# Block, partial-sum, low-part and latent-weight stores moved to GpSimd's queue, and another order of the three products of a block, in a two-layer decoder trunk

## The chip, the cores and the metric

The kernel runs on one core of one Trainium2 chip. The metric is the device time of one execution in microseconds, as the median of the runs shown. In the profile PE is TensorE's matmul, PEld its weight load, DVE is VectorE, ACT is ScalarE, POOL is GpSimd and SP is SyncE, which does nothing here but issue DMAs. PE and PEld share one sequencer.

## The reference

A decoder trunk of two layers works on 1024 tokens of width 1024, in float32. Layer 0 mixes with an mLSTM, layer 1 with latent attention on a shared latent K/V; each mixer is followed by an MLP with a squared ReLU and hidden width 4096. Every sub-block is wrapped in RMS norms, a shift and scale that a conditioning vector gives, and a gated residual. What the change touches most is the MLP and the latent projections:

```python
def sqrelu_mlp(h, w1, w2):
    return jnp.square(jax.nn.relu(h @ w1)) @ w2

def mla_shared_kv(x, shift, scale, g_in, w_a, g_latent, w_b, cos, sin):
    h = modulate(rmsnorm(x, g_in), shift, scale)
    kv = h @ w_a
    c_kv, k_rope = jnp.split(kv, [B_KV_LORA], axis=-1)
    ...
```

## The kernel before

**Split products.** A float32 operand is split into two float32r parts, a high part (a ScalarE copy) and a low part (a VectorE subtraction). `wsplit` (L199 to L206) does that for weights: L202 writes `wh`, L203 writes `wl`, both from the pool tag `ws` with 8 buffers. A product of 128 x 128 weights with 512 columns is then three matmuls into the same PSUM tile, made by `mm3` (L243): low-high (L244), high-low (L245), high-high (L246). Nearly all matrix work goes through `mm3`. Where the tokens' side is stationary (`up_rows`, and the mLSTM projections) `lh, ll` are parts of activations, elsewhere of weights.

**Buffers.** Raw weights come by DMA into the tag `raw` with only 4 buffers of 128 x 1024, each held until its split has read it. `k4` has 24 buffers and holds almost everything of that size, `tmp` has 3 buffers of 128 x 512, `ws` has 8. A buffer that a store reads is free only when the store has landed.

**Stages.** The 1024 tokens are two halves of 512. The first 470 us or so are the mLSTM layer. Then come the MLP of layer 0, the attention of layer 1 and its MLP, woven together. An MLP goes through its weights in three sweeps of 16 steps, so that the second half needs fewer products: a block of products is taken apart into sums, and partial results go through DRAM.

- Sweep 1 (`first`, L952): 128 x 512 of the first half's hidden values per step. The first half of its product is copied to `c` and stored to DRAM as the block sum `m` (L967, 256 KB).
- Sweep 2 (`second`, L976): per step two raw weight tiles are loaded (L983), and `m` is read back into `u` (L988). DVE makes sums and differences of the weights (L990, L991, L992, L997); L994 and L995 write the high and the low part `wv` of one of them, `wsplit` those of another, and the block of differences `o` is stored as `s` (L998, 512 KB). `hid` multiplies `wv` first (L1009), adds the result to `u` (L1010, with two more of the same kind), and stores the partial sums `u` (L1017, 512 KB).
- Sweep 3 (`third`, L1026) reads `s` and `u` back for the second half of the tokens.
- The down projection is `up_cols` (L1133) in layer 0 and `up_rows` in layer 1. `up_cols` stores the low part of its weights for the first half of the tokens as `lo` (L1156, 512 KB) and reads it back for the second half (L1168).
- `latent_weights` (L1327) runs beside layer 0's sweep 2, from about 700 to 830 us. For each of six blocks it loads a raw tile (L1337), accumulates a bias on DVE (L1341 to L1344), multiplies the tile by the gains (L1346), splits it, and stores high and low part as `lw` (L1351 or L1353, 512 KB each; half that for block 2). `latent` reads them back later.

So there are 32 stores each of `m`, `s`, `u` and `lo`, and 12 of `lw`: 140. All other stores of intermediate results stay on SP.

**What sets the order.** The kernel is written as Python generators that are interleaved by hand (`two_streams`, `weave`, `in_turn`). `go` chains them: with `tc.issue_after(last[0])` each piece's TensorE instructions are queued behind those of the piece before, so PE's order is nearly the program's. DVE, ACT, SP and POOL are ordered when the kernel is built: the framework plays the program through a timing model and puts an instruction into its engine's queue when the model has its inputs ready, by priority (`prompt` gives 300 steps of precedence). On the chip each queue then runs strictly in that order, and an instruction that waits holds back what is queued behind it.

```python
    def mm3(o, lh, ll, rh, rl, start, stop):
        nc.tensor.matmul(o, ll, rh, start=start, stop=False)
        nc.tensor.matmul(o, lh, rl, start=False, stop=False)
        pe_last[0] = nc.tensor.matmul(o, lh, rh, start=False, stop=stop)
    ...
                nc.scalar.copy(t[:, l_], r[0][:, l_])
                nc.vector.tensor_sub(t[:, r_], r[0][:, l_], t[:, l_].bitcast(F32))
                w = wsplit(r[1], 1024)
                nc.vector.tensor_sub(o[:, r_], r[0][:, r_], r[0][:, l_])
                nc.sync.dma_start(self.s[p_], o)
```

POOL has little to do before the change: nine small loads at the start (L275), memsets of single columns that claim accumulators (L173, waiting until the buffer is free), and memsets in the softmax (L1555).

Of the kernel before, what the change touches and what calls it, by code (L numbers as in the profile page):

```python
# [9 lines left out]
F32 = mybir.dt.float32  # L10
# [72 lines left out]
def kernel(  # L83
# [27 lines left out]
    nc = tc.nc  # L111
# [20 lines left out]
    def raw(dt=F32):  # L132
        return sb.tile([P, 1024], dt, tag="raw", bufs=RAW, name=f"raw_{next(uid)}")
# [13 lines left out]
    def ps():  # L147
        return pp.tile([P, 512], F32, tag="ps", bufs=2, name=f"ps_{next(uid)}")
# [89 lines left out]
    def wcols(w, c0, n=P, k0=0, nk=KD):  # L238
        return w[k0 * P : (k0 + nk) * P, c0 : c0 + n].rearrange("(k p) n -> p k n", p=P)

    pe_last = [None]

    def mm3(o, lh, ll, rh, rl, start, stop):  # L243
        nc.tensor.matmul(o, ll, rh, start=start, stop=False)  # L244
        nc.tensor.matmul(o, lh, rl, start=False, stop=False)  # L245
        pe_last[0] = nc.tensor.matmul(o, lh, rh, start=False, stop=stop)  # L246


    nc.scalar.preload_act_table_set("natural_log_exp_and_others")
# [672 lines left out]
    class Mlp:  # L922
# [29 lines left out]
        def first(self, p_, h):  # L952

            def load():
                r = raw()
                nc.sync.dma_start(
                    r.rearrange("p (a b) -> p a b", b=P), wcols(self.w1, p_ * P)
                )  # L960
                return wsplit(r, 1024)

            def hid(w):
                pt, c = ps(), tmp()
                self.product(pt, self.part(w, 0), h)
                evac(c, pt)
                nc.sync.dma_start(self.m[p_], c)  # L967
                yield "within"
                pt, s = ps(), tmp()
                self.product(pt, self.part(w, 1), h, 4)  # L970
                prompt(nc.vector.tensor_add)(s, c, pt)
                self.squares(0, p_, s)

            return prompt(load), hid

        def second(self, p_, ops):  # L976

            def load():  # L980
                r = [raw(), raw()]
                for i in range(2):
                    nc.sync.dma_start(  # L983
                        r[i].rearrange("p (a b) -> p a b", b=P),
                        wcols(self.w1, (p_ + NPR * i) * P),
                    )
                u, o = k4()[:, :1024], k4()[:, :1024]
                nc.sync.dma_start(u[:, :512], self.m[p_])  # L988
                l_, r_ = slice(0, 512), slice(512, 1024)
                nc.vector.tensor_add(o[:, l_], r[1][:, l_], r[1][:, r_])  # L990
                nc.vector.tensor_sub(r[1][:, l_], r[0][:, l_], r[1][:, l_])  # L991
                nc.vector.tensor_sub(r[0][:, l_], o[:, l_], r[0][:, l_])  # L992
                t = sb.tile([P, 1024], F32R, tag="ws", bufs=WS, name=f"wv_{next(uid)}")
                nc.scalar.copy(t[:, l_], r[0][:, l_])  # L994
                nc.vector.tensor_sub(t[:, r_], r[0][:, l_], t[:, l_].bitcast(F32))  # L995
                w = wsplit(r[1], 1024)
                nc.vector.tensor_sub(o[:, r_], r[0][:, r_], r[0][:, l_])  # L997
                nc.sync.dma_start(self.s[p_], o)  # L998
                return (t[:, l_], t[:, r_]), w, u

            def hid(ws):
                s2, w, u = ws
                u2, u3 = u[:, 0:512], u[:, 512:1024]
                if 4 not in ops:
                    ops[4] = half_op()
                    for k in range(4):
                        split_mod(ops[4].hi[k], ops[4].lo[k], ops["t4"][k], None)
                pt = ps()
                self.product(pt, s2, ops[2])  # L1009
                prompt(nc.vector.tensor_add)(u2, u2, pt)  # L1010
                if p_ and ops["later"]:
                    ops["later"].pop(0)()
                yield "within"
                pt = pc()
                self.product(pt, self.part(w, 0), ops[3])
                prompt(nc.vector.tensor_add)(u3, u2, pt)
                nc.sync.dma_start(self.u[p_], u)  # L1017
                yield "within"
                pt, s = ps(), tmp()
                self.product(pt, self.part(w, 1), ops[4])  # L1020
                prompt(nc.vector.tensor_add)(s, u3, pt)
                self.squares(0, NPR + p_, s)

            return prompt(load), hid

        def third(self, p_, ops, buf):  # L1026
# [106 lines left out]
        def up_cols(self, half, y, fs, i, last):  # L1133
            G, w2, hids = len(fs), self.w2, self.hids[half]
            n = KD // G

            def out(w):
                for m in range(i * n, (i + 1) * n, 2):
                    if m > i * n:
                        yield "within"  # L1140
                    b2, made = pm(), list(hids)
                    for j, q in enumerate(sorted(range(G), key=lambda q: made.index(fs[q]))):
                        for e in range(2):
                            c_ = ts(m + e - i * n, P)
                            mm3(
                                b2[:, e], w[0][:, q, c_], w[1][:, q, c_], *hids[fs[q]],
                                j == 0, j == G - 1,
                            )
                    self.accumulate((half, m + 1), y.t[m // 2], b2)

            views = [(a, 0, wcols(w2, i * n * P, n * P, f, r)) for a, f, r in self.runs(fs)]

            def load():
                if not half:
                    w = wload(views, n * P)
                    nc.sync.dma_start(self.lo[i][:, fs[0] : fs[0] + G], w[1].bitcast(F32))  # L1156
                    return w
                r = raw()
                w = [
                    sb.tile([P, 1024], F32R, tag="ws", bufs=WS, name=f"wk_{next(uid)}").rearrange(  # L1160
                        "p (a b) -> p a b", b=n * P
                    )
                    for _ in range(2)
                ]
                rv = r.rearrange("p (a b) -> p a b", b=n * P)
                for a, f, k in self.runs(fs):
                    nc.sync.dma_start(rv[:, a : a + k], wcols(w2, i * n * P, n * P, f, k))
                    nc.sync.dma_start(w[1][:, a : a + k].bitcast(F32), self.lo[i][:, f : f + k])  # L1168
                nc.scalar.copy(w[0], rv)
                return w  # L1170

            return prompt(load), out
# [151 lines left out]
    lw = scratch([6, 2, P, D], "lw")  # L1324
    lbias = const([P, 6 + 112], F32, "lbias")

    def latent_weights():  # L1327

        v = wcols(kv_w_a, 256, 64)
        views = [[(0, wcols(kv_w_a, m * P))] for m in range(2)] + [[(0, v), (64, v)]]  # L1330
        views += [[(0, wcols(b_w_q_a[0], m * P))] for m in range(3)]
        for b, vs in enumerate(views):
            A, sh = (Akv, kvada[:, 0:8]) if b < 3 else (Aq, adac(1, SH1))
            r_ = raw()
            r = r_.rearrange("p (a b) -> p a b", b=P)
            for c0, v in vs:
                nc.sync.dma_start(r[:, :, c0 : c0 + v.shape[2]], v)  # L1337
            yield
            acc = tma()[:, :P]
            with paced():  # L1340
                nc.vector.tensor_scalar(acc, r[:, 0], sh[:, 0:1], None, ALU.mult)  # L1341
                for k in range(1, KD):
                    nc.vector.scalar_tensor_tensor(
                        acc, r[:, k], sh[:, k : k + 1], acc, ALU.mult, ALU.add  # L1344
                    )
            nc.vector.tensor_mul(r, r, A.unsqueeze(2).to_broadcast([P, KD, P]))  # L1346
            for i, t in enumerate(wsplit(r_, D)):
                if b == 2:

                    f = lambda t: t.rearrange("p (a b) -> p a b", b=P)[:, :, ts(i, 64)]  # L1350
                    nc.sync.dma_start(f(lw[b, 0]), f(t).bitcast(F32))  # L1351
                else:
                    nc.sync.dma_start(lw[b, i], t.bitcast(F32))  # L1353
            yield "wait"
            pt = pc()
            nc.tensor.transpose(pt[:, :P], acc, ident)
            n = 64 if b == 2 else P
            nc.vector.reduce_sum(lbias[:n, b : b + 1], pt[:n, :P], axis=AX.X)
            if n < P:
                nc.vector.memset(lbias[n:P, b : b + 1], 0.0)  # L1360
# [797 lines left out]
    u = p0.scaled(xT0, (0,))  # L2158
# [28 lines left out]
    u = p1.scaled(xT0, (0, 1))  # L2187
# [18 lines left out]
    u = p2.scaled(xT0, (0, 1))  # L2206
# [387 lines left out]
```

## Time and profile before

| what | value |
|---|---|
| median of 3 runs (lowest to highest) | 2388.77 us (2384.43 to 2389.36) |
| profiled execution, its own time | 2390.72 us |
| its span, first to last instruction | 2388.9 us |
| mean granted TensorE clock | 0.985 |
| busy: PE, DVE, ACT, POOL | 2281.3, 1675.5, 1085.7, 17.6 us |
| DMA traffic | 482.03 MB, 202 GB/s over the span |

The profile is of one execution. Busy times are unions of an engine's instructions. A wait is charged to what ended last before the waiting instruction. A row of a timeline reads: start, duration, engine, line, operation, what it writes and reads, and in brackets the idle time of the engine just before with what ended it. A row of the waits reads: total in us, how many, the longest. A row of a stretch gives its length, then each engine's busy time and number of instructions, then the granted clock, the share of the DMA engines and GB/s. Matmuls overlap: one lasts about 0.39 us and the next starts well before it ends.

### The profile page before, as it was taken

How to read it: one execution, taken by the hardware profiler on the slowest of the kernel's cores; microseconds unless marked ns; L12 is line 12 of the kernel's file. 1: busy time of each engine (PE TensorE's matmuls, PEld its weight loads, DVE VectorE, ACT ScalarE, POOL GpSimd, SP SyncE). 2: the span in 40 equal slices, each digit the busy share in tenths (PEclk: the TensorE clock that was granted, in tenths of full speed). 3: DMA queues.
4: the chain of work that ended last, by engine and by line, in shares of the span. 5: the costliest groups of instructions: out<-in, count | busy, mean ns of one | idle time of the engine just before them, and what ended most of it. 6: DMA issues, size and time to landing. Idle time of an engine off the chain costs nothing.

```text
span 2388.9 us, 31122 instructions
## 1 busy us (share of the span) xinstructions
PE 2281.3 (95%) x11274; PEld 1886.1 (79%) x11274; DVE 1675.5 (70%) x2745; ACT 1085.7 (45%) x1811; POOL 17.6 (1%) x95
## 2 busy tenths in 40 slices
PE   8999999999998999999999989999999799999998
PEld 6888888887776788778878768878778688878887
DVE  6666767799887877767764787656648876666556
ACT  4364335574332335544444454534446333454433
POOL 1000000000000000000000000000000000000000
PEclk9999999999999999999999999999999899999999
DMA  9544455667998987655675774945246587675321
GB/s 319 171 131 123 150 151 158 190 210 240 300 280 256 297 270 273 210 185 176 194 242 160 268 236 135 323 166 187 104 138 233 151 275 224 222 262 187 115 90 69
DMA packets 406267, 482.03 MB, mean 202 GB/s; under 512 B 30468, under 2 KB 276289, under 8 KB 406113
## 3 DMA queue, kind: packets, MB, share of 16 engines
q1 hardware_dynamic: 405824, 479.94, 62.3%
q8 instruction: 89, 1.46, 0.3%
q14 instruction: 66, 0.53, 0.1%
q0 software_dynamic: 288, 0.10, 0.0%
HBM read 358.33 MB, written 121.63 MB: 201 GB/s over the span
## 4 chain that ended last, share of the span: by engine, by line
PE 73%; DVE 12%; DMA 9%; ACT 3%; issue 2%; SPq 1%; DVEq 0%; ACTq 0%
PE ps L244 12%; PE ps L245 12%; PE ps L246 12%; PE pm L244 8%; PE pm L245 8%; PE pm L246 8%; DMA raw<-in_mlp_w_dram 4%; DVE wl L203 2%; PE pc L245 2%; PE pc L244 2%; PE pc L246 2%; DVE k L211 1%; ACT wh L202 1%; DVE hd L458 1%; DVE tma L348 1%
## 5 line engine op out<-in xcount | busy, mean ns | idle before, releaser
L202 ACT CAST wh<-raw 128x1024 fp32r<-128x1024 f32 (+4 forms) x307 | 310.5, 1014 | 471.6 <-PE pm L245 119.8
L203 DVE TENSOR_TENSOR wl<-raw,wh 128x1024 fp32r<-128x1024 f32 (+4 forms) x307 | 360.9, 1178 | 220.8 <-ACT wh L202 198.8
L244 PE MATMUL ps<-k,wl 128*128 128x512 f32 x1100 | 436.7, 397 | 12.8 <-DVE wl L203 5.8
L245 PE MATMUL ps<-k,wh 128*128 128x512 f32 x1100 | 430.9, 392 | 1.5 <-DVE k L458 1.5
L246 PE MATMUL ps<-k,wh 128*128 128x512 f32 x1100 | 430.5, 391 | 0.0
L244 PEld LDWEIGHTS ps<-k,wl 128*128 128x128 f32 x1100 | 207.9, 189 | 61.6 <-DVE wl L203 7.3
L245 PEld LDWEIGHTS ps<-k,wh 128*128 128x128 f32 x1100 | 208.0, 189 | 46.0 <-DVE k L458 3.3
L246 PEld LDWEIGHTS ps<-k,wh 128*128 128x128 f32 x1100 | 207.6, 189 | 43.8
L244 PE MATMUL pm<-wh,hd 128*128 128x512 f32 x488 | 192.3, 394 | 9.8 <-DVE hd L458 8.9
L245 PE MATMUL pm<-wl,hd 128*128 128x512 f32 x488 | 190.8, 391 | 0.0
L246 PE MATMUL pm<-wh,hd 128*128 128x512 f32 x488 | 190.7, 391 | 0.0
L211 DVE TENSOR_TENSOR k<-k,pm 128x512 f32<-128x512 f32 (+1 forms) x170 | 141.3, 859 | 69.5 <-PE pm L246 69.3
L348 DVE SCALAR_TENSOR_TENSOR tma<-raw,cond,tma 128x512 f32<-128x512 f32 x168 | 125.9, 749 | 18.5 <-DMA raw<-in_ada_w_dram 9.9
L938 ACT ACTIVATE tmp<-tmp 128x512 f32<-128x512 f32 x80 | 50.5, 631 | 152.8 <-DVE tmp L211 133.9
L244 PEld LDWEIGHTS pm<-wh,hd 128*128 128x128 f32 x488 | 92.1, 189 | 30.5 <-DVE hd L458 9.7
L246 PEld LDWEIGHTS pm<-wh,hd 128*128 128x128 f32 x488 | 92.1, 189 | 19.3
L245 PEld LDWEIGHTS pm<-wl,hd 128*128 128x128 f32 x488 | 92.2, 189 | 19.1 <-issue 0.2
L244 PE MATMUL pm<-hd,wk 128*128 128x512 f32 x256 | 102.1, 399 | 0.3 <-ACT hd L457 0.3
L245 PE MATMUL pm<-hd,wk 128*128 128x512 f32 x256 | 100.6, 393 | 1.2 <-DVE hd L458 1.2
L246 PE MATMUL pm<-hd,wk 128*128 128x512 f32 x256 | 100.1, 391 | 0.0
L244 PE MATMUL pm<-hd,wl 128*128 128x512 f32 x256 | 99.8, 391 | 0.0
L245 PE MATMUL pm<-hd,wh 128*128 128x512 f32 x256 | 99.7, 389 | 0.0
(442 smaller groups left out, 4671.7 us busy)
## 6 DMA issues: line engine op xcount, KB each, us to landing
raw<-in_mlp_w_dram SPq DMA_DIRECT2D x156, 512.0 KB, 4.7
raw<-in_ada_w_dram SPq DMA_DIRECT2D x80, 512.0 KB, 4.6
raw<-in_mlp_w_dram SPq DMA_DIRECT2D x136, 256.0 KB, 4.6
raw<-in_a_w_in_dram SPq DMA_DIRECT2D x44, 512.0 KB, 4.7
lo<-wl SPq DMA_DIRECT2D x32, 512.0 KB, 5.6
s<-k SPq DMA_DIRECT2D x32, 512.0 KB, 3.3
u<-k SPq DMA_DIRECT2D x32, 512.0 KB, 4.8
raw<-s SPq DMA_DIRECT2D x32, 512.0 KB, 4.0
```

The costliest lines, as they stand in the source:

```text
L202: nc.scalar.copy(hi[:, :n], r[:, :n])
L203: i = nc.vector.tensor_sub(lo[:, :n], r[:, :n], hi[:, :n].bitcast(F32))
L211: return f(*a, **k)
L244: nc.tensor.matmul(o, ll, rh, start=start, stop=False)
L245: nc.tensor.matmul(o, lh, rl, start=False, stop=False)
L246: pe_last[0] = nc.tensor.matmul(o, lh, rh, start=False, stop=stop)
L348: nc.vector.scalar_tensor_tensor(acc, r[:, kk], cond[:, k : k + 1], acc, ALU.mult, ALU.add)
L458: nc.vector.tensor_sub(lo, u, hi.bitcast(F32))
L938: nc.scalar.activation(s, s, AF.Relu)
```

## The change

The three products of `mm3` are issued as high-high, high-low, low-high. The stores of `m`, `s`, `u`, `lo` and `lw` are issued by GpSimd in place of SyncE. Nothing else is edited; the order of instructions on each engine is worked out again when the kernel is built.

```diff
     def mm3(o, lh, ll, rh, rl, start, stop):
-        nc.tensor.matmul(o, ll, rh, start=start, stop=False)
+        nc.tensor.matmul(o, lh, rh, start=start, stop=False)
         nc.tensor.matmul(o, lh, rl, start=False, stop=False)
-        pe_last[0] = nc.tensor.matmul(o, lh, rh, start=False, stop=stop)
+        pe_last[0] = nc.tensor.matmul(o, ll, rh, start=False, stop=stop)
...
                 evac(c, pt)
-                nc.sync.dma_start(self.m[p_], c)
+                nc.gpsimd.dma_start(self.m[p_], c)
...
                 nc.vector.tensor_sub(o[:, r_], r[0][:, r_], r[0][:, l_])
-                nc.sync.dma_start(self.s[p_], o)
+                nc.gpsimd.dma_start(self.s[p_], o)
...
                 prompt(nc.vector.tensor_add)(u3, u2, pt)
-                nc.sync.dma_start(self.u[p_], u)
+                nc.gpsimd.dma_start(self.u[p_], u)
...
                     w = wload(views, n * P)
-                    nc.sync.dma_start(self.lo[i][:, fs[0] : fs[0] + G], w[1].bitcast(F32))
+                    nc.gpsimd.dma_start(self.lo[i][:, fs[0] : fs[0] + G], w[1].bitcast(F32))
...
-                    nc.sync.dma_start(f(lw[b, 0]), f(t).bitcast(F32))
+                    nc.gpsimd.dma_start(f(lw[b, 0]), f(t).bitcast(F32))
                 else:
-                    nc.sync.dma_start(lw[b, i], t.bitcast(F32))
+                    nc.gpsimd.dma_start(lw[b, i], t.bitcast(F32))
```

## The prediction

> **What bounds the kernel now.** I read the busy times first, then who ended PE's waits, then the stretches in which they lie.
>
> ```profile
> span 2388.9 us, 31122 instructions
> PE 2281.3 (95%) x11274; PEld 1886.1 (79%) x11274; DVE 1675.5 (70%) x2745; ACT 1085.7 (45%) x1811; POOL 17.6 (1%) x95
> ```
>
> PE is the bound; all that an edit can win lies in the 2388.9 - 2281.3 = 107.6 us in which it is idle, and in matmuls that run at a lower clock. The waits of PE, three rows that the order of products touches, and the same kind within 540 to 840 us:
>
> ```profile
> PE ps L244 <- DVE wv L995: 19.9, 8, 5.0
> PE pm L244 <- DVE hd L458: 8.9, 2, 7.7
> ...
> PE ps L244 <- DVE wl L203: 5.8, 4, 2.6
> ```
> ```profile
> PE ps L244 <- DVE wv L995: 15.8, 7, 5.0
> ```
>
> L244 is the low-high product, the first of a block today. These are 14 waits, 34.6 us, in which PE stands at the first product for a low part that DVE has not yet written. Seven of the eight at `wv` lie in sweep 2 of layer 0. That stretch beside sweep 2 of layer 1 (busy PE, PEld, DVE, ACT, POOL; clock; DMA share; GB/s):
>
> ```profile
> 690.00:830.00 140.00, 123.52 (x504) 99.34 (x505) 109.55 (x177) 42.29 (x59) 0.00 (x0) 0.94 0.88 275
> ...
> 1885.00:2090.00 205.00, 202.63 (x902) 165.65 (x903) 143.14 (x208) 79.79 (x116) 0.39 (x4) 0.99 0.78 246
> ```
>
> In 690 to 830 us, where the latent weights run beside sweep 2, PE idles 16.5 us of 140 at clock 0.94, with the DMA engines busy 0.88 of the time. In layer 1's sweep 2, with the same stores of `s` and `u`, PE idles 2.4 us of 205. So `s` and `u` can matter in the first stretch only, and there `lo` and `lw` join them.
>
> **The order of the products.** No instruction is added or removed. High-high needs only what ACT writes, and the weight's low part moves from the first to the third product. What that is worth is the distance from a block's first to its third matmul:
>
> ```profile
> 731.75 0.50 PE L244 MATMUL ps<-k,wv 128*128 128x512 f32 x1 [1.26 <-DVE wv L995]
> 732.09 0.39 PE L245 MATMUL ps<-k,wv 128*128 128x512 f32 x1
> 732.32 0.40 PE L246 MATMUL ps<-k,wv 128*128 128x512 f32 x1
> ```
>
> The third starts 0.57 us after the first. How long DVE takes over a low part, and how many steps the stretch of 690 to 830 us has:
>
> ```profile
> L203 DVE TENSOR_TENSOR wl<-raw,wh x23: 1207/1222/1227, 692.0 to 822.7; 128x1024 fp32r<-128x1024 f32 x23
> ...
> L995 DVE TENSOR_TENSOR wv<-raw,wv x9: 674/685/687, 691.4 to 819.6; 128x512 fp32r<-128x512 f32 x9
> L990 DVE TENSOR_TENSOR k<-raw x9: 683/692/693, 694.9 to 827.7; 128x512 f32<-128x512 f32 x9
> ```
>
> The two products ahead can now run while DVE writes the low part, as that subtraction (0.69 to 1.22 us) always follows the copy that made the high part. So each of the 14 waits shrinks by at most 0.57 us. Two are shorter than that:
>
> ```profile
> 786.07 0.50 PE L244 MATMUL ps<-k,wv 128*128 128x512 f32 x1 [0.52 <-DVE wv L995]
> ```
> ```profile
> 1090.90 0.50 PE L244 MATMUL ps<-k,wl 128*128 128x512 f32 x1 [0.32 <-DVE wl L203]
> ```
>
> With these, the upper end is 12 x 0.57 + 0.84 = 7.7 us. The lower end is nothing: if the low part's arrival is set by DMA and DVE alone, a block that ends sooner makes the next wait longer. A loss I exclude: PE's order is chained by the program, high-high never waits longer than low-high did, and a block's last product comes no later.
>
> A wait also costs clock. Two more waits at `wv`, and the stretches just after four of them:
>
> ```profile
> 692.10 0.79 PE L244 MATMUL ps<-k,wv 128*128 128x512 f32 x1 [2.21 <-DVE wv L995]
> ```
> ```profile
> 769.93 0.50 PE L244 MATMUL ps<-k,wv 128*128 128x512 f32 x1 [2.14 <-DVE wv L995]
> ```
> ```profile
> 820.39 0.50 PE L244 MATMUL ps<-k,wv 128*128 128x512 f32 x1 [1.39 <-DVE wv L995]
> ```
> ```profile
> 692.00:695.40 3.40, 3.30 (x8) 2.62 (x9) 2.42 (x6) 0.00 (x0) 0.00 (x0) 0.51 0.95 262
> ...
> 731.80:735.20 3.40, 3.40 (x15) 2.82 (x16) 3.11 (x4) 2.00 (x4) 0.00 (x0) 1.00 1.00 281
> ...
> 770.60:774.00 3.40, 3.40 (x10) 2.63 (x9) 1.55 (x2) 0.00 (x0) 0.00 (x0) 0.50 1.00 264
> ...
> 820.50:824.00 3.50, 3.50 (x16) 2.84 (x17) 3.50 (x5) 0.38 (x1) 0.00 (x0) 1.00 0.93 248
> ```
>
> After gaps of 2.21 and 2.14 us PE ran 3.4 us at half clock, a loss of 1.7 us each; after 1.26 and 1.39 us it did not. Shortened by 0.57 us, the first two become 1.64 and 1.57 us, nearer to those that cost nothing: up to 3.4 us more. The Trainium skill, page "TensorE: Matmul & The Clock Gate", section "Why this matters for your kernels", puts the limit at idle gaps of about 3 us; by that neither gap would have cost clock and this term would be 0. The rows differ, so they decide.
>
> I keep the six full gains and the 0.32 us outside the stretch (6 x 0.57 + 0.32 = 3.7 us), half of the 6 x 0.57 + 0.52 = 3.9 us inside it (2.0), and one of the two clock episodes (1.7). Sum: **-7.4 us**, between 0 and -11.1.
>
> **The stores.** Of the instructions, 140 DMA issues leave SP's queue and enter POOL's. What SP and the loads do in 690 to 830 us, and how `s` and the weight loads fare over the whole run:
>
> ```profile
> SPq L998 <- DVE k L997: 22.8, 6, 5.5
> ...
> SPq L983 <- DVE wl L203: 6.6, 7, 1.7
> ```
> ```profile
> L998 SPq DMA_DIRECT2D s<-k x32: 319/332/595, 656.3 to 2071.4; - x32
> ...
> DMA to landing us min/median/max: 2.6/3.3/5.9
> ```
> ```profile
> L983 SPq DMA_DIRECT2D raw<-in_mlp_w_dram x64: 367/384/3057, 644.8 to 2061.6; - x64
> ...
> DMA to landing us min/median/max: 4.0/6.0/8.5
> ```
>
> SP does stand before the store of `s`, 22.8 us here. But the weight load behind it waits for a `raw` buffer that `wl` (L203) and L997 themselves release, on the same engine within a microsecond or so. Taking the stores away therefore lets SP arrive sooner at a load that mostly cannot yet be issued. SP's own time, 140 x 0.332 = 46 us, lies beside PE's work. I take nothing for it; the bounds are below. Loads land 2.0 us later in the median than at best, part of it behind stores in the same queue; with stores elsewhere they share the engines, so the bytes ahead stay about the same, at 0.88 busy. The gain lies between 0 and what that delay costs (rival 2).
>
> On the other side stands a later landing. No store on POOL is in this trace; the nearest rows are its loads at the start, and short DMAs of SP:
>
> ```profile
> 1.28 0.70 POOL L275 DMA_DIRECT2D raw<-in_norm_g_dram  x1 [0.34 <-issue]
> ...
> 6.09 0.50 POOL L275 DMA_DIRECT2D raw<-in_a_gate_b_dram  x1
> ```
> ```profile
> raw<-in_b_w_q_b_dram SPq DMA_DIRECT2D x16, 96.0 KB, 2.5
> ...
> inv<-in_inv_freq_dram SPq DMA_DIRECT2D x4, 0.1 KB, 6.6
> ...
> raw<-in_norm_g_dram POOLq DMA_DIRECT2D x1, 32.0 KB, 3.9
> ...
> raw<-in_a_gate_b_dram POOLq DMA_DIRECT2D x1, 0.1 KB, 5.2
> ```
>
> POOL spends 0.5 to 0.7 us per DMA: 140 of them make about 100 us of an engine that is busy 17.6. Landing takes 3.9 to 5.2 us for next to no data, against 2.5 us on SP for more: 1.4 to 2.7 us later. But in the same crowded start SP's tiny load took 6.6 us, so the excess may be below zero as well. What hides it are DVE's waits on the loads, in 690 to 830 us:
>
> ```profile
> DVE k L990 <- DMA raw<-in_mlp_w_dram: 12.8, 7, 4.1
> ...
> DVE k L990 <- DMA s<-k: 1.0, 1, 1.0
> ```
>
> L990 writes `o` into a `k4` buffer that a landed store has freed, and starts the chain to `wv`. In the nine steps it waits seven times for the load (1.8 us each), once for a store. A store that lands up to 1.8 us later mostly hides behind the load. Between the two ends I take **0** for the stores, as the load's wait is the nearest row.
>
> **The sum.** The profiled execution took 2390.7 us, 1.8 us around its span: 2390.7 - 7.4 = 2383.3. The median of the runs shown is 1.95 us below that execution, which gives 2381.4. I forecast **2382**, about 0.3% faster than 2388.8. A difference under 0.2%, 4.8 us, is about what cannot be told from none: faster is below 2384.0, slower above 2393.6.
>
> **The rivals.**
>
> 1. *Stores land late (slower).* The place is L990, and the splits that need a `ws` buffer from `lw`, in 690 to 830 us. At 2.7 us late, beyond the 1.8 us of cover, seven steps lose 0.9 and two lose 2.7: 11.7 us, and about three more waits pass into half clock, 5.1. Less 3.7 for the order outside: +13. At 2.05 us late the same makes 5.9 + 3.4 - 3.7 = +5.6. Price +9: **2398**. It decides once a store lands more than some 1.8 us later than now. For it: POOL's landings of 3.9 to 5.2. Against it: 6.6 on SP at the same time, and 202.63 of 205 in layer 1. The Trainium skill, "SBUF — State Buffer", section "SBUF: two separate sides", speaks against the change here: descriptors of a DMA that GpSimd issues cannot be written while VectorE runs an operation on both ports. No run here shows it yet.
> 2. *Loads land sooner.* With 2.0 us of queueing shortened, half of the 12.8 us goes (6.4) and half of the clock lost there, 0.06 x 140 / 2 = 4.2; with the order's 3.7 and 2.0 that is -16: **2373**. Against it: `raw` buffers set when a load may start.
> 3. *All absorbed.* Inside the stretch everything waits for loads; the stores do nothing, and only 3.7 us remain: **2385**. The Trainium skill, "DMA: Bandwidth & Descriptors", section "Issuing engines are not separate DMA queues", says that another issuing engine saves only sequencer time, which fits this rival's half on the stores.
> 4. *The rebuilt order is worse.* In 540 to 840 us one row shows how a queue's order costs:
>
> ```profile
> ACT wh L202 <- DVE raw L1346: 26.0, 3, 14.0
> ```
>
> ACT stands at a latent weight's split while the copy for `wv` may be queued behind it. Two such places more would cost about two waits of 5 us: +8, **2397**.
>
> **How the numbers follow.** Forecast 0.32, rival 1 0.24, rival 2 0.14, rival 3 0.18, rival 4 0.12. Faster are the forecast and rival 2, 0.46; within 0.2% is rival 3, 0.18; slower are rivals 1 and 4, 0.36. The range runs from below rival 2 to the +13 of rival 1: 2369 to 2402. The likeliest case alone runs from 2377.7 (-11.1) to 2384.
>
> **What would show it.** For the order: L244's waits at `wv` and `wl` fall by about 0.57 us each, reappearing on the third product, and fewer stretches at half clock follow. For rival 1: more and longer waits of L990 for `s` and `u`, and landings of the POOL stores well above 3.3 us. For rival 2: L983 lands nearer to 4 us and L990 waits less for loads. For rival 3: the same idle time in 690 to 830 us. The forecast fails if the idle time of PE moves elsewhere than at these lines, above all if ACT or DVE stands in another order.

## The result and the profile after

The changed kernel took **2379.31 us** (median of 5 runs, 2375.46 to 2383.9) beside 2388.84 us for the kernel before (5 runs, 2384.43 to 2391.41): ratio 0.996, 95% interval 0.9941 to 0.9978. A second set of 10 runs gave 2380.07 us and 0.9964 (0.9952 to 0.9975). The forecast was 2382, the range 2369 to 2402. The profiled execution took 2383.9 us, 6.8 less than the profiled one before, and is the slowest of its five: its rows show where waits lie, the medians what they are worth.

The page's header, busy times and DMA queues:

```profile
span 2382.1 us, 31220 instructions
...
PE 2285.4 (96%) x11274; PEld 1886.2 (79%) x11274; DVE 1676.6 (70%) x2745; ACT 1084.1 (46%) x1811; POOL 93.2 (4%) x235
...
q1 hardware_dynamic: 383872, 415.44, 54.1%
q0 software_dynamic: 18272, 64.60, 7.7%
```

Span minus PE's busy time is 96.7 us, against 107.6 before. POOL carries 140 more instructions and 75.6 us more, 0.54 us each, with the 64.50 MB of the stores now in its own queue (64.60 MB with its small loads). The waits of PE, by line and releaser (us in total, times, longest):

```profile
PE ps L244 <- ACT wv L994: 8.8, 4, 3.7
...
PE pm L246 <- DVE hd L458: 7.2, 1, 7.2
...
PE ps L246 <- DVE wv L995: 4.8, 4, 2.2
...
PE ps L244 <- ACT wh L202: 1.7, 2, 0.9
...
PE pm L244 <- ACT hd L457: 1.0, 2, 0.7
...
PE ps L246 <- DVE wl L203: 0.8, 2, 0.5
...
PE pm L246 <- DVE wl L203: 0.3, 1, 0.3
```

No wait of the first product for a low part of these groups is left. PE now stops first for the high part (L994, L202, L457, all ACT) and again at the third product for the low part. The 34.6 us of before have become 24.6, 10.0 less: more than the bound of 7.7, since some waits shrank for other reasons (one is traced below). Against it, the second product's waits for the low part of an activation (L245 behind `k` of L458) grew from 6.0 to 8.2 us. The stretch of sweep 2 with the latent weights beside it, then sweep 2 of layer 1, shifted as the markers shifted (us; busy PE, PEld, DVE, ACT, POOL; granted clock; DMA share; GB/s):

```profile
690.00:830.00 140.00, 125.72 (x517) 99.78 (x517) 109.34 (x176) 43.20 (x59) 20.96 (x39) 0.94 0.86 277
...
1877.00:2082.00 205.00, 201.68 (x894) 165.23 (x895) 141.87 (x205) 78.27 (x113) 16.40 (x35) 0.98 0.78 245
```

PE idles 14.3 us of the first instead of 16.5, at the same clock of 0.94 and nearly the same DMA share. DVE's waits there, and the landing of the weight loads of L983 over the run:

```profile
DVE k L990 <- DMA raw<-in_mlp_w_dram: 21.4, 7, 6.6
...
DVE k L990 <- DMA s<-k: 0.4, 1, 0.4
```
```profile
DMA to landing us min/median/max: 3.9/6.0/12.6
```

Loads didn't land sooner: the median is 6.0 as before, the latest 12.6 instead of 8.5, and L990 waits 21.4 us for them instead of 12.8. Nor do the stores of `s` hold it up.

### The profile page after: what moved, and what is told of

It reads as the page before. It is cut to its first block, busy times and chain, and to the rows that moved or that the text cites. A ratio compares the mean times of both kernels' runs of the same rounds, so it can differ in the third digit from the quotient of the medians.

```text
span 2382.1 us, 31220 instructions
## 1 busy us (share of the span) xinstructions
PE 2285.4 (96%) x11274; PEld 1886.2 (79%) x11274; DVE 1676.6 (70%) x2745; ACT 1084.1 (46%) x1811; POOL 93.2 (4%) x235
## 3 DMA queue, kind: packets, MB, share of 16 engines
q0 software_dynamic: 18272, 64.60, 7.7%
## 4 chain that ended last, share of the span: by engine, by line
PE 67%; issue 15%; DVE 7%; DMA 6%; ACT 2%; POOL 2%; SPq 1%; POOLq 0%; DVEq 0%; ACTq 0%
PE ps L245 11%; PE ps L244 11%; PE ps L246 11%; PE pm L244 7%; PE pm L245 7%; PE pm L246 7%; DMA raw<-in_mlp_w_dram 3%; PE pc L245 1%; PE pc L246 1%; PE pc L244 1%; DMA raw<-s 1%; PE pc L1646 1%; PE pm L791 1%; PE pm L1545 1%; DVE wl L203 1%
## 5 line engine op out<-in xcount | busy, mean ns | idle before, releaser
L202 ACT CAST wh<-raw 128x1024 fp32r<-128x1024 f32 (+4 forms) x307 | 310.6, 1015 | 508.1 <-PE pm L245 144.6
L244 PE MATMUL ps<-k,wh 128*128 128x512 f32 x1100 | 438.3, 399 | 8.5 <-ACT tmp L938 3.4
L245 PE MATMUL ps<-k,wh 128*128 128x512 f32 x1100 | 432.2, 393 | 2.8 <-DVE k L458 2.8
L246 PE MATMUL ps<-k,wl 128*128 128x512 f32 x1100 | 431.9, 393 | 0.8 <-DVE wl L203 0.8
L245 PEld LDWEIGHTS ps<-k,wh 128*128 128x128 f32 x1100 | 208.6, 190 | 47.3 <-DVE k L458 4.4
L245 PE MATMUL pm<-wl,hd 128*128 128x512 f32 x488 | 190.7, 391 | 0.0
L245 PEld LDWEIGHTS pm<-wl,hd 128*128 128x128 f32 x488 | 92.0, 189 | 19.1 <-issue 0.2
L245 PE MATMUL pm<-hd,wk 128*128 128x512 f32 x256 | 100.3, 392 | 0.6 <-DVE hd L458 0.6
```

Source lines behind the costliest of these rows:

```text
L202: nc.scalar.copy(hi[:, :n], r[:, :n])
L244: nc.tensor.matmul(o, lh, rh, start=start, stop=False)
L246: pe_last[0] = nc.tensor.matmul(o, ll, rh, start=False, stop=stop)
```

## The experiments

Twelve kernels were run, each timed beside the kernel before (K0; the changed kernel is K1). "Idle" is span minus PE's busy time of the one profiled execution (the expectations from the third set on count only what lies ahead of a matmul, some 7 us less). "Clock" is the mean over the runs of span x (1 - granted clock), "net" the rest of the span, i.e. what a full clock would have left. PE goes through its blocks of products in the same order in all kernels, so the time from one matmul to another, counted from the first (matmul 0), compares the same work; such counts are from the one profile of each kernel, and the two of K1 differ by up to 1.5 us in the stretches named below.

| kernel | median us | ratio to K0 (95%) | idle | net | clock |
|---|---|---|---|---|---|
| K0 | 2387.95 (29 runs of one set) | 1 | 107.6 | 2351.3 | 35.0 |
| K1, both sets | 2379.31, 2380.07 | 0.996, 0.9964 | 96.7, 95.7 | 2344.9 | 32.5 |
| order only | 2383.21 | 0.9978 (0.9965-0.9991) | 98.8 | 2345.4 | 36.3 |
| stores only | 2387.9 | 1.000 (0.9987-1.0013) | 106.8 | 2351.3 | 34.6 |
| low-high first, high-low last | 2384.16 | 0.9984 (0.9975-0.9993) | 100.3 | 2347.4 | 34.9 |
| K1, latent stores on SyncE | 2388.08 | 1.0002 (0.9993-1.0011) | 101.5 | 2350.4 | 36.2 |
| order + latent stores | 2378.29 | 0.9958 (0.9942-0.9974) | 93.8 | 2344.1 | 31.8 |
| order + `s`, `u` | 2388.92 | 0.9998 (0.9986-1.0009) | 99.9 | 2349.2 | 37.8 |
| order + `m` | 2381.72 | 0.9967 (0.9955-0.998) | 93.5 | 2348.5 | 30.0 |
| order + `m` + latent stores | 2377.36 | 0.9955 (0.9941-0.9969) | 92.7 | 2343.4 | 33.3 |
| order in the MLP's up projection only | 2390.3 | 1.001 (0.9998-1.0023) | 105.0 | 2352.7 | 35.2 |
| order everywhere else only | 2388.35 | 0.9998 (0.9988-1.0008) | 103.7 | 2348.6 | 37.3 |
| K1, high-low last outside the up projection | 2388.18 | 1.0006 (0.9995-1.0018) | 108.0 | 2352.7 | 34.2 |

K0's net and clock are means over 85 runs of all three sets, the other kernels' over 5 to 12 each (K1 15). The clock is listed to three digits, so the last two columns are good to about 1 us where there are 10 runs or more, less with five to eight.

**Order only.** All stores go back to SyncE.

```diff
-                nc.gpsimd.dma_start(self.m[p_], c)
+                nc.sync.dma_start(self.m[p_], c)
...
```

> The order of products alone (high-high, high-low, low-high); all stores stay on SyncE. Theory O (the order makes the gain, the stores nothing): 2379 to 2382 us, ratio 0.995 to 0.997, and the waits of the first product for wv and wl gone as in the changed kernel. Theory S (the stores make most of it, since loads land sooner): 2385 us, ratio 0.998 to 0.999. Theory R (the engines' rebuilt order makes it, by chance): anywhere between 2378 and 2395.

Measured 0.9978: 5.3 us faster, within 2.1 to 8.4. That lies between the first two theories, so by itself it doesn't decide. Its waits of PE:

```profile
PE ps L244 <- ACT wv L994: 8.9, 5, 3.4
PE ps L246 <- DVE wv L995: 8.6, 7, 1.9
...
PE pm L246 <- DVE hd L458: 7.2, 1, 7.2
...
PE ps L244 <- ACT wh L202: 1.7, 2, 0.9
...
PE pm L244 <- ACT hd L457: 1.0, 2, 0.7
...
PE ps L246 <- DVE wl L203: 0.3, 1, 0.3
```

Together 27.7 us, 6.9 less than 34.6. At `wv` 17.5 us are left of 19.9, so 2.4 went where 8 waits could give up to 4.5: PE waits for ACT's high part first and for the low part behind it. At `wl` 3.8 us went, where the 0.57 us of the prediction allows 2.0. The reason is one wait, the longest there:

```profile
576.22 0.80 PE L244 MATMUL ps<-k,wl 128*128 128x512 f32 x1 [2.64 <-DVE wl L203]
```

It hung on a raw load: ACT, which makes the high part, stood 2.94 us for it before; with the order alone that is 0.87 us, and PE doesn't stop there. From matmul 3200 to 3300 (562 to 589 us) K0 took 26.7 us, the stores alone 28.1 and the control below 26.5, all with low-high first; the other eleven profiles took 22.7 to 23.9 us. Among them is the kernel in which this very product keeps the old order (23.3 us). So the largest piece of the order's gain that can be placed, some 3 to 4 us with the clock, is for the most part not the 0.57 us of a shifted product.

**Stores only.** The body of `mm3` goes back to low-high, high-low, high-high; all 140 stores stay on GpSimd.

> The stores alone on GpSimd, products in the old order. Theory O: 2388 us, ratio 0.999 to 1.001. Theory S: 2380 to 2383 us, ratio 0.996 to 0.998, with the weight loads of L983 landing 1 us or more sooner. Late landing (stores that land later hold up L990 or a split): 2391 to 2395 us, ratio 1.001 to 1.003.

Measured 1.000, with net and clock as before. Neither sooner loads nor late landing shows in the time, though the loads of L983 landed in 5.4 us in the median instead of 6.0: by themselves the stores are worth nothing, as forecast. But the next kernels show that stores have effects of both signs. (The profile of this kernel is of the slowest of its twelve runs, 2395.96 us.)

**Control: low-high stays first.**

```diff
         nc.tensor.matmul(o, ll, rh, start=start, stop=False)
-        nc.tensor.matmul(o, lh, rl, start=False, stop=False)
-        pe_last[0] = nc.tensor.matmul(o, lh, rh, start=False, stop=stop)
+        nc.tensor.matmul(o, lh, rh, start=False, stop=False)
+        pe_last[0] = nc.tensor.matmul(o, lh, rl, start=False, stop=stop)
```

> Control for the rebuilt order: low-high stays first, only the two products behind it change places (low-high, high-high, high-low), all stores on SyncE. The part that PE waits for first is the same. Theory O: 2387 to 2390 us, ratio within 0.001 of 1, with the 20 us of waits for wv at the first product as before. Theory R: moves by 4 us or more either way, with other places of waiting.

Measured 0.9984, 3.8 us faster: more than theory O allows and just short of theory R's 4 us, with the waits at `wv` as before (18.9 us). So 0.57 us at each late weight isn't the only thing that a new order of products does. Part of it may be the low part of an activation: the second product's waits for it (L245 behind `k` of L458, 6.0 us before) become 2.3 us at the third. The rest may be the rebuilt order of the other engines: 73 of DVE's 2745 instructions stand elsewhere in its sequence than in K0, and 123 in the kernel with the order alone, though the edits change no instruction of DVE.

**The latent weights' stores back on SyncE.** The expectation says 14 stores, and so does a later one; there are 12.

```diff
-                    nc.gpsimd.dma_start(f(lw[b, 0]), f(t).bitcast(F32))
+                    nc.sync.dma_start(f(lw[b, 0]), f(t).bitcast(F32))
                 else:
-                    nc.gpsimd.dma_start(lw[b, i], t.bitcast(F32))
+                    nc.sync.dma_start(lw[b, i], t.bitcast(F32))
```

> The changed kernel with the stores of the latent weights (14 of 140) back on SyncE; s, u, m and the low parts stay on GpSimd. Theory O: 2379 us as the changed kernel, ratio 0.995 to 0.997. If the later landing of the latent weights' stores costs something (three splits wait 1.6 to 4.5 us each for such a store in the changed kernel, not before): 2374 to 2377 us, and these three waits shorter.

Both expectations fell: the kernel lost the whole gain (1.0002). The waits that such stores cause in K1 (4.5 us of ACT at one `wv`, below) were no cost worth removing:

```profile
ACT wv L994 <- DMA lw<-wh: 4.5, 1, 4.5
```

The loss lies beside sweep 2: from matmul 3300 to 4400 (589 to 870 us) this kernel took 288.6 us, K1 282.3 and 280.8, K0 281.2. What differs most there is SyncE's queue from 640 to 900 us. In turn, the order alone, this kernel, and K1 (what SyncE stood before, behind what; us, times, longest):

```profile
SPq L998 <- DVE k L997: 42.0, 12, 7.0
...
SPq L1353 <- ACT wh L202: 5.2, 3, 2.7
```
```profile
SPq L1353 <- ACT wh L202: 46.2, 5, 9.9
...
SPq L983 <- DVE wv L995: 22.4, 5, 6.3
```
```profile
SPq L1337 <- DVE wl L203: 41.4, 5, 10.4
SPq L983 <- DVE wv L995: 30.4, 8, 7.4
```

With all stores on SyncE it stands before the store of `s`, and when it comes to the latent store that one is nearly ready: 5.2 us. Take `s` and `u` away, and SyncE comes early to the latent store (L1353), whose high part ACT hasn't written, and stands there for 46.2 us with the weight loads behind it. Take that away too, and it stands before a load (L1337) that waits for a buffer. The time at the head of the queue stays; only what it is spent on changes. That this is the cause of the loss is likely but not shown: DVE's waits at L990 for the loads did not grow (26.4 us in 640 to 900 us, K1 30.4 and 28.2), and 47 of its instructions stand elsewhere in its sequence than in K1.

**The second set.** K1 once more:

> The changed kernel once more, unaltered, in more runs beside the others: order alone gave 0.9978 and stores alone 1.000, together 0.996 in five runs. If the two parts simply add: 2382 to 2384 us, ratio 0.997 to 0.9985. If they help each other: 2378 to 2380 us, ratio 0.995 to 0.9965.

0.9964: the two parts help each other, by some 4 us over their sum (3.9 by the mean spans, with 3.1 of uncertainty either way). The latent stores alone on GpSimd, with the order:

> Order of products changed and only the 14 stores of the latent weights on GpSimd; s, u, m and the low parts on SyncE. With the latent weights alone back on SyncE the time was 2388. If these 14 stores are what counts among the 140: 2378 to 2380 us, ratio 0.995 to 0.997. If they count nothing and the spread comes from the rebuilt order (theory R): about the order alone, 2382 to 2385, or 2388 as with the others moved.

0.9958, the gain of K1 with 12 of its 140 stores. Beside the order alone, PE's busy time in 640 to 900 us (order alone first, this kernel second) rises by 4.6 us at the same clock, so that many us of idle time are gone there:

```profile
sum 260.00, PE 242.57 PEld 196.00 DVE 199.66 ACT 88.58 POOL 0.27; mean PE 242.57 PEld 196.00 DVE 199.66 ACT 88.58 POOL 0.27
```
```profile
sum 260.00, PE 247.21 PEld 200.31 DVE 205.01 ACT 90.04 POOL 7.42; mean PE 247.21 PEld 200.31 DVE 205.01 ACT 90.04 POOL 7.42
```

From matmul 3300 to 4400 it took 276.8 us, and the kernel with `m` moved as well 277.5, against 282.9 with the order alone. But K1 doesn't have this gain (282.3 and 280.8), although its latent stores are on GpSimd too, and the control has it (276.6) with every store on SyncE. So it isn't shown that a freer queue brings it; another sequence of the engines can do the same.

**Where the order's gain lies.** In one kernel only `product`, the MLP's up projection, calls the new `mm3`, and every other place, the down projection too, a copy with the old order; the reverse came in the third set. The expectation below takes all waits at `wv` and `wl` to lie in `product`; three of the four at `wl` don't.

> The new order of products in the MLP's blocks alone (the function product), low-high first everywhere else, all stores on SyncE. Theory O (the gain lies at the waits for wv and wl, which are all in these blocks): the gain of the order alone, 2382 to 2385 us, ratio 0.997 to 0.9985. Theory R (the rebuilt order of the engines makes it, by chance): anything between 2380 and 2392, with no likeness to the order alone.

> The reverse of the kernel with the order changed in the MLP's blocks alone: high-high first everywhere else, low-high first in the MLP, all stores on SyncE. If the order's gain lies outside the MLP (attention and latent blocks): idle time 92 to 95 us, 2383 to 2386 us, ratio 0.998 to 0.999. If it lay at wv and wl in the MLP: idle time 98 us or more, 2387 to 2390 us.

1.001 and 0.9998: neither half brings what the whole does (0.9978). So neither the theory that puts the gain at `wv` and `wl`, nor its opposite, was borne out. Both lie within the wide range of theory R. Idle time falls by 2.6 and 3.9 us in the two profiles, together 6.5 of the 8.8 of the whole, but the medians don't follow (the second profile is of the fastest of its eleven runs).

**High-low last where it is late.** Everywhere outside `product`:

```diff
+    def mm3_rl(o, lh, ll, rh, rl, start, stop):
+        nc.tensor.matmul(o, lh, rh, start=start, stop=False)
+        nc.tensor.matmul(o, ll, rh, start=False, stop=False)
+        pe_last[0] = nc.tensor.matmul(o, lh, rl, start=False, stop=stop)
```

> The changed kernel, but each block ends with the part that is late there: low-high last in the MLP's blocks, as in the change, high-low last in all others, where the changed kernel's second product waits for the low part of an activation (L245 behind L458, 6.8 us in five waits). Theory O: 0.3 us less at each of these waits, 1 to 3 us below the changed kernel. Theory R: no such tie, 4 us or more either way.

A miss: 1.0006, some 8 us slower than K1. PE's waits for `k` of L458 fell from 8.2 only to 7.0 us, and PE waited 12.2 us instead of 7.1 in K1 for DVE's sums ahead of the transposes of the modulation columns. That points to another order of DVE's work rather than to the products; it wasn't tried apart.

**Which stores.** On top of the order, `m` alone, `s` and `u` alone, and `m` with the latent weights:

> Order of products changed, only the 32 stores of m on GpSimd. Theory V: the wait of L244 for L457 at 1420 us falls from 4.2 us to under 0.5, as in all kernels with m on GpSimd so far, the rest as with the order alone: idle time about 87 us, 2378 to 2381 us, ratio 0.9955 to 0.997. If that wait hangs on another of the stores: 4.2 us as before and 2383.

> Order of products changed, only the 64 stores of s and u on GpSimd. Theory V: SyncE no longer stands at L998, but at the latent weights' stores instead (L1353 behind L202, 46 us with m, s, u and the low parts moved), so the loads behind gain nothing: idle time 91 to 94 us, 2383 to 2388 us, ratio 0.998 to 1.000. The rival of the prediction that loads land sooner: 2375 to 2380.

> Order of products changed, the stores of the latent weights and of m on GpSimd; s, u and the low parts on SyncE. Theory V (each kernel's time is its busy time plus PE's idle time plus the clock lost, the latter some 32 to 39 us whatever the edit; lw on GpSimd takes 4.5 us of idle time in 640 to 900 us, m on GpSimd takes the 4.2 us wait of L244 for L457 at 1420 us): idle time 82 to 83 us, 2373 to 2376 us, ratio 0.993 to 0.995, below the changed kernel. Theory R (rebuilt order by chance): 2378 to 2388.

With `m` the expectation held: 0.9967, below the order alone by 1.5 us in the medians and 3.2 in the mean spans, with five runs. The kernel with `s` and `u` on GpSimd, and the one with `m` there, where eight tiles are scaled (L908) and shifted (L911) for the next block (DVE's timeline of both; between them PE's largest wait of the first in 1400 to 1430 us):

```profile
1416.93 2.73 DVE L908 SCALAR_TENSOR_TENSOR k<-k,mods,tmc 128x512 f32<-128x512 f32 x4
1419.58 0.69 DVE L458 TENSOR_TENSOR hd<-tmp,hd 128x512 fp32r<-128x512 f32 x1
1420.18 2.73 DVE L908 SCALAR_TENSOR_TENSOR k<-k,mods,tmc 128x512 f32<-128x512 f32 x4
1422.83 1.29 DVE L911 TENSOR_TENSOR k<-k,k 128x512 f32<-128x512 f32 x2
```
```profile
PE ps L244 <- ACT k L457: 4.2, 1, 4.2
```
```profile
1413.67 2.08 DVE L908 SCALAR_TENSOR_TENSOR k<-k,mods,tmc 128x512 f32<-128x512 f32 x3
...
1417.45 0.74 DVE L908 SCALAR_TENSOR_TENSOR k<-k,mods,tmc 128x512 f32<-128x512 f32 x1
1418.12 0.69 DVE L911 TENSOR_TENSOR k<-k,k 128x512 f32<-128x512 f32 x1
```

With `m` on SyncE, DVE scales all eight tiles before it adds to the first; with `m` on GpSimd the first half goes ahead, and PE's 4.2 us are gone. This wait, of 3.6 to 4.2 us, stands in all seven profiles with `m` on SyncE; in the seven with it on GpSimd at most 0.3 us of it is left. The time follows: from matmul 6800 to 7200 (1396 to 1501 us) the seven with `m` on SyncE take 103.5 to 106.5 us, the seven with it on GpSimd 100.5 to 102.4. No data flow asks for the wait: moving a store changed the sequence that the program builds for DVE. Here K1 gains on the order alone (101.2 and 100.5 us against 106.4), and in its profiles nowhere else by as much.

With `s` and `u` alone, 0.9998: 4.8 us slower than the order alone by the ratios, and SyncE stands before the latent store again:

```profile
SPq L1353 <- ACT wh L202: 40.7, 5, 9.4
```

But PE loses little beside it: from matmul 3300 to 4400 this kernel took 283.9 us, the order alone 282.9. Where the rest of the loss lies stays open.

With `m` and the latent weights 0.9955, a little above what was expected (0.993 to 0.995), its idle time 85 us in the expectation's count, where 82 to 83 was expected. It can't be told from K1 (0.9960 and 0.9964) or from the latent stores alone (0.9958).

## Why the prediction was right or wrong

**Sign and size** were right. 2379.3 and 2380.1 lie 2 to 3 us below 2382, and the likeliest case's own range, 2377.7 to 2384, held both. In part that was luck: the order alone brought 5.3 us where 7.4 were summed up, and the stores beside it some 4 where 0 was put.

**The order of products, waits** (-3.7 outside, -2.0 inside the stretch). The sum came out near, not its parts: with the order alone PE's waits for late parts fell by 6.9 us where 5.7 were kept and 7.7 was the upper end, and the net time by 5.9. But at `wl` more went than a shifted product can give, with one load that came sooner, and at `wv` about half of what it could. In and around the stretch little survives: PE was busy 243.4 of the 260 us from 640 to 900 before and 242.6 with the order alone, and behind the wait at 576 us, from matmul 3300 to 4400, the order alone was 1.6 us slower. The halves of the edit don't add up either. The copy that makes the high part sets the first product's start; the step "the two products ahead can now run while DVE writes the low part" left out that PE then waits for ACT.

**The order of products, clock** (-1.7). With the order alone the clock's loss didn't fall: 36.3 us against 35.0. In K1 it is 2.5 lower, about the 1.7 of the forecast, but the order by itself doesn't show it. The reading that a gap of 2.2 us costs and one of 1.4 doesn't was right; which gap costs depends on more than its length (below).

**The stores** (0). Right as measured alone (1.000), wrong as reasoned. Beside the order they bring some 4 us, and the 0 hides terms of some 5 us of both signs that don't add up: `s` and `u` alone lose 4.8 us; the latent stores on GpSimd take 4.6 us of idle time away in 640 to 900 us as long as `s` and `u` stay on SyncE, by the queue or by the rebuilt sequence; `m` there takes a wait of 4.2 us away through DVE's order, and this is the one that K1's profiles keep. Two steps failed. Taking the stores away was to let SyncE arrive sooner "at a load that mostly cannot yet be issued": with the latent stores left on SyncE it arrived at one of them first and stood there 46.2 us instead of 5.2; only with all of them gone does it stand before loads, as the sentence says. And the rebuilt sequence of the other engines stood only in rival 4, not in this term, where moving `m` brought some 4 us by it.

**Rival 1** (late landing) fell: L990 waits 0.4 us for a store, though stores do land later, by 0.2 to 1.8 us in the median. **Rival 2** (sooner loads) fell: median landing 6.0 both times. **Rival 3** (all absorbed, 2385) was near on `wv` in the stretch, but its share of the stores rested on their changing nothing. The Trainium skill, "DMA: Bandwidth & Descriptors", section "Issuing engines are not separate DMA queues", counts only sequencer time as saved by another issuing engine. Here it also decided what stood at the head of SyncE's queue: the two kernels with `s` and `u` but not the latent weights moved, in which that was a latent store, are 5 to 9 us slower than their neighbours, though in only one of them does the loss lie at that place. **Rival 4** (the rebuilt order) was right as a mechanism, with either sign: 4.2 us won at L457, 5.1 us of waits more at the transposes of one kernel.

**Still open**: why the order in the up projection and outside it bring nothing apart; why the stores bring nothing with the old order, although the wait at L457 is gone there too; and what the stores of `lo` do, which were never moved alone. Each kernel rebuilds the sequence of all engines, with effects as large as those looked for. A kernel with the old sequence frozen and only the products exchanged would tell; it wasn't tried.

## What to carry to other kernels

When a transfer leaves an in-order queue, look at the next instruction in that queue that isn't ready: it takes over the wait. Beside the new order, moving some of the stores was worse than moving none or all. Where a program rebuilds the order of every engine after an edit, expect effects of some 4 us in 2388 from that alone, compare the engines' sequences before explaining such a difference, and run a control. Split a difference into time at full clock and time lost to the clock before looking for it in waits; and where one engine's order is fixed, count its instructions to find where two kernels part.

## What the runs showed of the hardware

**The clock is set on a raster of 3.41 us.** Between the ends of the span, half clock comes in stretches of 3.41, 6.83 or 10.24 us whose starts, within a run, lie whole multiples of 3.41 us apart. Two windows before the change, with the window behind each (columns as above; PE's busy time, then the granted clock after POOL):

```profile
729.63:733.05 3.42, 2.16 (x11) 1.51 (x10) 3.03 (x3) 3.42 (x6) 0.00 (x0) 1.00 0.71 266
733.05:736.46 3.41, 3.41 (x17) 2.82 (x16) 3.16 (x5) 0.76 (x2) 0.00 (x0) 1.00 1.03 266
767.18:770.59 3.41, 1.27 (x7) 0.78 (x6) 3.41 (x5) 1.93 (x3) 0.00 (x0) 1.00 0.99 267
770.59:774.01 3.42, 3.42 (x10) 2.65 (x9) 1.56 (x2) 0.00 (x0) 0.00 (x0) 0.50 0.99 264
774.01:777.42 3.41, 3.41 (x17) 2.80 (x16) 1.87 (x6) 0.00 (x0) 0.00 (x0) 1.00 1.17 299
```

1.26 us idle in a window: the next one runs at full clock. 2.14 us idle: the next one runs at half. In K1, with 1.94 us idle:

```profile
762.46:765.87 3.41, 1.47 (x6) 0.62 (x4) 3.41 (x7) 2.48 (x3) 0.43 (x2) 1.00 0.99 269
765.87:769.28 3.41, 3.38 (x8) 2.71 (x9) 3.30 (x6) 0.04 (x1) 0.76 (x2) 0.50 0.76 180
```

Over the 14 profiles, without the first 50 and the last 10 us, behind a window at full clock with less than 1.4 us idle, half clock followed 0 times of 8975; with 1.4 to 2.0 us, 51 of 133; with more than 2.0, 128 of 128. (In the first 50 us it came four times behind 0.6 to 0.9 us; why isn't shown.) A gap that falls across the edge of two windows can escape: in K0 one of 2.39 us at 1406.9 us lies with 1.94 and 0.45 us in two windows, and full clock followed; in K1 one of 2.18 us at 1875.3 us lies in a single window, and half clock followed. That may be why the clock's loss differs from run to run: for K0 over 85 runs its standard deviation is 3.8 us, that of the spans 3.4. The Trainium skill, "TensorE: Matmul & The Clock Gate", section "Part 1: The HAM clock gate (the "warmup" mystery)", states a free-running window of 3413 ns, which these starts show; of its half clock after an idle window, the runs show that 2.0 of the 3.41 us are enough.

**A store from GpSimd** cost POOL 0.53 us (`s`: 531 to 553 ns over 32) while DVE was busy around it, so nothing here shows its descriptors held up. It landed later than from SyncE by 0.2 to 1.1 us in the median (`s` 4.0 against 3.3, `u` 5.0 against 4.8, `m` 4.3 against 3.5, the low parts `lo` 6.7 against 5.6), and by 1.8 us for the low parts of the latent weights (6.0 against 4.2, five stores):

```profile
lo<-wl POOLq DMA_DIRECT2D x32, 512.0 KB, 6.7
s<-k POOLq DMA_DIRECT2D x32, 512.0 KB, 4.0
u<-k POOLq DMA_DIRECT2D x32, 512.0 KB, 5.0
```
